# Input loads in turns, a second group of idle matmuls, and transposes tied between matmuls, in a two-layer SGU and retention trunk

## The chip, the cores and the metric

The kernel runs on one core of a Trainium2 chip. The metric is the device time of one execution in microseconds, as the median of three runs. One profiled execution of the same program gives the trace that is read here; its times are counted from the start of its span. PE is the matrix engine with its own weight loads beside it, DVE the vector engine, ACT the scalar engine, POOL the GpSimd engine, and SP the engine whose queue issues most DMAs.

## What is computed

A trunk of two layers over 512 rows (tokens) of 1024 columns in float32. Layer 0 mixes with a spatial gating unit, layer 1 with retention over four heads, and each is followed by a feed-forward layer (FFN) with SwiGLU of hidden width 2816. Every mixer and FFN sees a normed copy of the stream.

```python
def rmsnorm(x, g):
    return x * lax.rsqrt(jnp.mean(x * x, axis=-1, keepdims=True) + EPS) * g

def sgu_mixer(h, w_in, w_s, b_s, ln_g, ln_b, w_out):
    z = jax.nn.gelu(h @ w_in)
    u, v = jnp.split(z, 2, axis=-1)
    v = layernorm(v, ln_g, ln_b)
    ...                                    # causal mixing inside chunks of 128 rows
    return (u * mixed) @ w_out

def swiglu(h, w_gu, w_down):
    a, b = jnp.split(h @ w_gu, 2, axis=-1)
    return (jax.nn.silu(a) * b) @ w_down

def reference(x, ...):
    h = x
    for i in range(DEPTH):                 # DEPTH = 2
        hn = rmsnorm(h, mix_norm_g[i])
        h = h + (sgu_mixer(hn, ...) if i == 0 else retention(hn, ...))
        h = h + swiglu(rmsnorm(h, ffn_norm_g[i]), ffn_w_gu[i], ffn_w_down[i])
    return rmsnorm(h, final_norm_g)
```

## The kernel before

**Precision and tiles.** The 512 rows are four chunks `c` of 128. A float32 operand of a large matrix product is split into a high part, its value rounded to the matrix engine's fast float32 type (fp32r), and a low part, the rest. A product is then three matmuls into one sum: high times high, high times low, low times high (`three`, L246 to L249). For a weight tile (two blocks of 128 rows by 512 columns) `halves` (L209) makes the high part `wh_` on ACT (L216, L219) and the low part `wl_` on DVE (L223, L226) from the raw tile `wr_` that SP loads (`fetch_tile`, L201). In the first mixer these steps also multiply by the norm's weights, which have to stand as columns: `rows_to_cols` (L190) transposes rows by one matmul against an identity and copies the result on DVE. `mix0` is such a set of columns for the first norm, `gains` a set for later uses.

**Activations.** `turn` (L665) turns a chunk: eight transposes of 128 by 128 on PE (L669) into PSUM, then the high part `XH_` on ACT (L673) and the low part `XL_` on DVE (L674), both over 128 x 1024.

**Opening.** Five idle matmuls (`wake`, L176) run on PE before any data is there; the profile shows each as two instructions. Then x's chunks arrive in halves of 256 KB (`load_x`, L783), and the first product is `v0`, the first 512 columns of v: four steps `i` over pairs of blocks of the depth, four chunks `c`, each pair of `c` and step six matmuls of 512 columns, 96 in all. The products don't wait for the norm's factor per row: it is applied at the gelu (L827), so the squares of x (`square_in`, L787) and a chain of small DVE operations (`rsqrt_cols`) have to be done only by then. After v0 come v1, the other half of v, and u0 and u1.

**FFN.** Products of FFN and output are formed by a scheme with seven block products in place of eight (`seven`, L321), whose products P1, P7, P6, Q4, P5, P2, P3 run in an order given by hand. P1 and P7 come first; each needs a weight sum and an activation sum. In an FFN the raw weights of P6 come out of those of P7 by an accumulating DMA on POOL's queue, and then get their high and low parts like any tile. The first product, P1, needs chunks of rows that the norm before has only just made: with `between`, the job that turns the fourth chunk (`late_one`) runs behind step 0 of P1, and the jobs in `between` come behind P1's last step. `turn_late` (L689) turns a chunk with high priority.

**What sets the order.** `pipeline` runs a list of jobs and starts the loading, high and low steps of a job a fixed number of jobs ahead (FETCH 8, HIGH 6, PREP 5). A scheduler then orders each engine's instructions by their dependences and priority, so the order on an engine isn't that of the code; `tc.issue_after(instruction)` ties what stands in it behind an instruction. An engine takes its own instructions strictly in its order, and SP issues loads in its order.

The functions that the change touches, as they stand:

## Time and profile before

| what | us |
|---|---|
| median of three runs | 1203.94 |
| the runs, lowest to highest | 1203.91 to 1204.99 |
| the profiled execution | 1203.29 |
| its span (first to last instruction) | 1201.5 |
| PE busy | 1184.5 (99%) |
| DVE busy | 924.1 (77%) |
| ACT busy | 643.7 (54%) |
| POOL busy | 160.8 (13%) |

Busy time says how long an engine had an instruction in work, not whether it worked at full speed: matmuls are pipelined, and the granted clock (PEclk, as a share of the full 2.4 GHz; 0.50 is 1.2 GHz) is listed by stretch. A row of a timeline gives start, duration and instruction, and behind it in brackets how long the engine stood idle before it and what released it. Lines (L669) are those of the kernel before.

### The profile page before, as it was taken

The numbers are of one execution on the slowest core, as the hardware profiler recorded it, in microseconds if no ns is written. First come the engines' busy times: TensorE is split into PE (matmuls) and PEld (weight loads), VectorE is DVE, ScalarE is ACT, GpSimd is POOL, SyncE is SP. The second block draws the span as 40 slices with busy tenths as digits, with TensorE's granted clock in tenths as the row PEclk, the third lists the DMA queues.
The fourth block names the chain that finished last, engine by engine and source line by source line (L and its number), as shares of the span: only waits on it lengthen the run. The fifth ranks groups of instructions, "written<-read, shape, count | busy, mean of one in ns | idle before, by whom it ended". The sixth has DMA issues, their size and how long they took to land.

```text
span 1201.5 us, 18058 instructions
## 1 busy us (share of the span) xinstructions
PE 1184.5 (99%) x7206; PEld 1062.8 (88%) x7206; DVE 924.1 (77%) x1095; ACT 643.7 (54%) x815; POOL 160.8 (13%) x143
## 2 busy tenths in 40 slices
PE   8999999999999999999999999999999999999997
PEld 7888899998999988988888888888899989999986
DVE  5587968698987789787674757879768797666897
ACT  5523755454444547555453645566556554455465
POOL 1000120111110130201101001130121111101210
PEclk9999999999999999999999999999999999999999
DMA  9912968767876788766566457878866788677792
GB/s 314 281 52 54 246 133 206 180 162 216 203 204 145 202 176 266 182 139 172 115 186 145 120 132 170 205 129 282 220 140 173 180 223 221 153 192 191 151 243 99
DMA packets 118980, 216.42 MB, mean 180 GB/s; under 512 B 7496, under 2 KB 20848, under 8 KB 118896
## 3 DMA queue, kind: packets, MB, share of 16 engines
q1 hardware_dynamic: 83888, 148.13, 36.9%
q0 software_dynamic: 34720, 66.61, 33.1%
q8 instruction: 56, 0.92, 0.3%
q10 hardware_dynamic: 288, 0.52, 0.1%
q14 instruction: 28, 0.23, 0.1%
HBM read 212.10 MB, written 2.10 MB: 178 GB/s over the span
## 4 chain that ended last, share of the span: by engine, by line
PE 86%; issue 5%; DMA 4%; DVE 3%; ACT 2%; POOL 1%; SPq 0%; DVEq 0%; POOLq 0%; ACTq 0%
PE X_gu L249 6%; PE X_gu L248 6%; PE X_gu L247 6%; PE Y_gu L248 3%; PE Y_gu L249 3%; PE Y_gu L247 3%; PE X_dn L247 3%; PE X_dn L248 3%; PE X_dn L249 3%; PE X_vg L247 2%; PE X_vg L248 2%; PE X_vg L249 2%; PE ps_qk L247 2%; PE ps_qk L248 2%; PE ps_qk L249 2%
## 5 line engine op out<-in xcount | busy, mean ns | idle before, releaser
L223 DVE TENSOR_TENSOR wl_gu_P<-wr_gu_P,wh_gu_P 128x1024 fp32r<-128x1024 f32 x120 | 144.6, 1220 | 45.1 <-ACT wh_gu_P L216 44.9
L216 ACT ACTIVATE wh_gu_P<-wr_gu_P 128x1024 fp32r<-128x1024 f32 x120 | 122.7, 1052 | 66.2 <-DVE wr_gu_P L375 34.7
L347 POOL DMA_DIRECT2D wr_gu_P<-in_ffn_w_gu x48 | 58.4, 1258 | 381.3 <-DMA wr_gu_P<-in_ffn_w_gu 167.3
L216 ACT ACTIVATE wh_dn_P<-wr_dn_P 128x1024 fp32r<-128x1024 f32 x72 | 69.3, 981 | 51.7 <-DMA wr_dn_P<-in_ffn_w_down 13.3
L223 DVE TENSOR_TENSOR wl_vg_P<-wr_vg_P,wh_vg_P 128x1024 fp32r<-128x1024 f32 x48 | 58.3, 1220 | 34.9 <-ACT wh_vg_P L216 28.7
L223 DVE TENSOR_TENSOR wl_dn_P<-wr_dn_P,wh_dn_P 128x1024 fp32r<-128x1024 f32 x72 | 79.5, 1130 | 3.2 <-issue 2.2
L347 POOL DMA_DIRECT2D wr_vg_P<-in_ret_w_in x26 | 31.5, 1250 | 262.7 <-DMA wr_vg_P<-in_ret_w_in 79.2
L347 POOL DMA_DIRECT2D wr_dn_P<-in_ffn_w_down x36 | 42.0, 1242 | 179.5 <-DMA wr_dn_P<-in_ffn_w_down 92.3
L216 ACT ACTIVATE wh_vg_P<-wr_vg_P 128x1024 fp32r<-128x1024 f32 x48 | 49.6, 1055 | 28.5 <-DMA wr_vg_P<-in_ret_w_in 13.6
L248 PE MATMUL ps_qk<-XL_r,wh_qk 128*128 128x512 f32 (+1 forms) x160 | 55.6, 348 | 0.0
L247 PE MATMUL ps_qk<-XH_r,wh_qk 128*128 128x512 f32 (+1 forms) x160 | 55.3, 348 | 0.0
L249 PE MATMUL ps_qk<-XH_r,wl_qk 128*128 128x512 f32 (+1 forms) x160 | 55.1, 348 | 0.0
L248 PE MATMUL Y_gu<-xP7l_f,wh_gu_P 128*128 128x256 f32 x160 | 45.4, 284 | 0.4 <-DVE xP7l_f L743 0.4
L248 PE MATMUL X_gu<-XL_f,wh_gu_P 128*128 128x256 f32 x160 | 45.4, 283 | 0.0
L249 PE MATMUL X_gu<-XH_f,wl_gu_P 128*128 128x256 f32 x160 | 45.3, 283 | 0.0
L247 PE MATMUL X_gu<-xP6h_f,wh_gu_P 128*128 128x256 f32 x160 | 45.3, 283 | 0.0
L248 PE MATMUL X_gu<-xP6l_f,wh_gu_P 128*128 128x256 f32 x160 | 45.3, 283 | 0.0
L249 PE MATMUL X_gu<-xP6h_f,wl_gu_P 128*128 128x256 f32 x160 | 45.3, 283 | 0.0
L247 PE MATMUL Z_gu<-XH_f,wh_gu_P 128*128 128x256 f32 x160 | 45.3, 283 | 0.0
L248 PE MATMUL Z_gu<-XL_f,wh_gu_P 128*128 128x256 f32 x160 | 45.3, 283 | 0.0
L249 PE MATMUL Z_gu<-XH_f,wl_gu_P 128*128 128x256 f32 x160 | 45.3, 283 | 0.0
L247 PE MATMUL X_gu<-xP5h_f,wh_gu_P 128*128 128x256 f32 x160 | 45.3, 283 | 0.0
(590 smaller groups left out, 4206.8 us busy)
## 6 DMA issues: line engine op xcount, KB each, us to landing
wr_gu_P<-in_ffn_w_gu SPq DMA_DIRECT2D x100, 512.0 KB, 4.8
wr_dn_P<-in_ffn_w_down SPq DMA_DIRECT2D x50, 512.0 KB, 4.9
wr_gu_P<-in_ffn_w_gu POOLq DMA_DIRECT2D x48, 512.0 KB, 7.6
wr_vg_P<-in_ret_w_in SPq DMA_DIRECT2D x40, 512.0 KB, 5.0
wr_dn_P<-in_ffn_w_down POOLq DMA_DIRECT2D x30, 512.0 KB, 7.4
wr_vg_P<-in_ret_w_in POOLq DMA_DIRECT2D x26, 512.0 KB, 7.4
wr_ro_P<-in_ret_w_out SPq DMA_DIRECT2D x20, 512.0 KB, 5.6
wr_qk<-in_ret_w_in SPq DMA_DIRECT2D x32, 256.0 KB, 3.1
```

Source lines behind the costliest of these rows:

```text
L216: nc.scalar.activation(h, s, AF.Copy)
L223: nc.vector.tensor_tensor(l, s, f32(h), ALU.subtract)
L247: nc.tensor.matmul(o, ah, bh, start=start, stop=False, skip_group_check=True)
L248: nc.tensor.matmul(o, ah, bl, start=False, stop=False, skip_group_check=True)
L249: return nc.tensor.matmul(o, al, bh, start=False, stop=stop, skip_group_check=True)
L347: nc.gpsimd.dma_start(raw[p, 0, g, s][:, 0:nk, :], source(b, g, s, nk), accum_op=ALU.add)
```

## The change

It does five things.

- In the opening, x's chunks and v0's weight tiles are issued on SP in turns: chunk 0, tile 0, chunk 1, tile 1, and so on, in sixteen DMAs of 256 KB. Before, tile 0 came behind chunk 0, then came chunks 1 to 3, and tiles 1 to 3 followed behind another small load, as three DMAs of 512 KB.
- Ten more idle matmuls (WAKE2) are tied behind the transpose of the `mix0` weights.
- In v0's loop the order in the code changes: a step turns its chunk first, takes the earlier tiles for it, and then the new tile for all chunks so far.
- All four squares are made on ACT behind that loop. Before, the first was made on DVE, and each stood in the loop.
- In `seven`, with `between`, the matmuls of P1's step 1 for the first chunk of a pair are tied behind the last transpose that `turn` issued. This holds in both FFNs.

```diff
+WAKE2 = 10
...
+    def keep_awake(n, after=None):
+
+        wake = PS("wake")
+        for _ in range(n):
+            with tc.issue_after(after.ins) if after else nullcontext():
+                after = nc.tensor.matmul(wake[:, 0, 0:P], ones, ones, start=True, stop=True)
+        done(wake)
+
+    keep_awake(WAKE)
...
-        nc.tensor.transpose(ps[:, 0, 0:n], rows_in[name], ident[0:n, 0:n])
+        xn["turned"] = nc.tensor.transpose(ps[:, 0, 0:n], rows_in[name], ident[0:n, 0:n])
...
                 for c in range(2):
-                    matmuls(p, g, s, nk, c)
+                    with tc.issue_after(xn["turned"].ins) if between and i == 1 and c == 0 else nullcontext():
+                        matmuls(p, g, s, nk, c)
...
-            nc.tensor.transpose(ps[:, k, :], src[:, k * P:(k + 1) * P], ident)
+            xn["turned"] = nc.tensor.transpose(ps[:, k, :], src[:, k * P:(k + 1) * P], ident)
...
     def square_in(c):
-        sq = G(f"xq{c}", F32, (P, D))
-        if c == 0:
-            nc.vector.scalar_tensor_tensor(sq, X[:, c, :], 1.0, X[:, c, :], ALU.mult, ALU.mult, accum_out=ss2[:, c:c + 1])
-        else:
-            nc.scalar.activation(sq, X[:, c, :], AF.Square, accum_out=ss2[:, c:c + 1])
+        nc.scalar.activation(G(f"xq{c}", F32, (P, D)), X[:, c, :], AF.Square, accum_out=ss2[:, c:c + 1])
 
     load_rows(nc.gpsimd, "mix0", mix_g[0:1])
-    load_x(0)
-    v0w = [None] * NC
-    wr = G("wr_v0_0")
-    for a in range(2):
-        nc.sync.dma_start(wr[:, a, :], w_in[a * P:(a + 1) * P, D:D + T])
+    raw0 = []
+
+    def load_w0(kp):
+        raw0.append(G(f"wr_v0_{kp}"))
+        for a in range(2):
+            k = 2 * kp + a
+            nc.sync.dma_start(raw0[kp][:, a, :], w_in[k * P:(k + 1) * P, D:D + T])
+
+    for what, i in ((load_x, 0), (load_w0, 0), (load_x, 1), (load_w0, 1), (load_x, 2), (load_w0, 2), (load_x, 3), (load_w0, 3)):
+        what(i)
+    done(turn(0, X[:, 0, :], "in"))
     mix0_col = rows_to_cols("mix0")
-    done(turn(0, X[:, 0, :], "in"))
+    keep_awake(WAKE2, xn["turned"])
     vps = [PS(f"ps_v0_{i}") for i in range(2)]
+    v0w = []
     for i in range(NC):
         if i > 0:
-            wr = fetch_tile(f"v0_{i}", w_in, 2 * i, 2, ((D, T),))
-        if i + 1 < NC:
-            load_x(i + 1)
-        v0w[i], high, low = halves(wr, f"v0_{i}", 2, [mix0_col(2 * i + a) for a in range(2)])
+            done(turn(i, X[:, i, :], "in"))
+            for kp in range(i):
+                natural_step(vps[i // 2][:, i % 2, :], i, kp, v0w[kp])
+        parts, high, low = halves(raw0[i], f"v0_{i}", 2, [mix0_col(2 * i + a) for a in range(2)])
         high()
         low()
-        for c in range(i):
+        v0w.append(parts)
+        for c in range(i + 1):
             natural_step(vps[c // 2][:, c % 2, :], c, i, v0w[i])
-        for kp in range(i + 1):
-            natural_step(vps[i // 2][:, i % 2, :], i, kp, v0w[kp])
-        square_in(i)
-        if i + 1 < NC:
-            done(turn(i + 1, X[:, i + 1, :], "in"))
+    for c in range(NC):
+        square_in(c)
```

What that makes of the engines' orders is shown at three places. In these rows `x8` counts like instructions in a row, and a name's last number tells one buffer from another.

PE at the very start, before the change. `xT_in_0` to `xT_in_3` are the transposes of x's four chunks, `mix0_ps` that of the norm's weights, `ps_v0_0` and `ps_v0_1` the sums of v0, `wh_v0_0` and `wl_v0_0` the parts of its first weight tile:

```order
L176 MATMUL wake_89<-ones_81 128x128 x5
L669 MATMUL xT_in_0_108<-ident_76,X_95 128x128 x8
L193 MATMUL mix0_ps_104<-ident_76,mix0_rows_97 128x8
L669 MATMUL xT_in_1_139<-ident_76,X_95 128x128 x8
L247 MATMUL ps_v0_0_121<-wh_v0_0_125,XH_in_117 128x512
L669 MATMUL xT_in_2_180<-ident_76,X_95 128x128 x8
L248 MATMUL ps_v0_0_121<-wl_v0_0_126,XH_in_117 128x512
```

And with the change:

```order
L181 MATMUL wake_89<-ones_81 128x128 x5
L677 MATMUL xT_in_0_119<-ident_76,X_95 128x128 x8
L200 MATMUL mix0_ps_132<-ident_76,mix0_rows_97 128x8
L181 MATMUL wake_136<-ones_81 128x128 x10
L677 MATMUL xT_in_1_161<-ident_76,X_95 128x128 x8
L254 MATMUL ps_v0_0_147<-wh_v0_0_149,XH_in_128 128x512
L677 MATMUL xT_in_2_196<-ident_76,X_95 128x128 x4
L255 MATMUL ps_v0_0_147<-wl_v0_0_150,XH_in_128 128x512
```

The ten idle matmuls stand ahead of the second chunk's transposes. The first four transposes of the third chunk still stand behind one matmul of v0, as all eight did.

DVE around the gains, before the change (`wl_v0_1` to `wl_v0_3` are low parts of v0's tiles, `gains_cols` the columns of the gains):

```order
L226 SCALAR_TENSOR_TENSOR wl_v0_1_155<-wr_v0_1_150,mix0_cols_106,wh_v0_1_154 128x512 x2
L195 COPY gains_cols_331<-gains_ps_329 128x32
L674 TENSOR_TENSOR XL_in_118<-xT_in_3_233,XH_in_117 128x8x128
L226 SCALAR_TENSOR_TENSOR wl_v0_2_196<-wr_v0_2_191,mix0_cols_106,wh_v0_2_195 128x512 x2
L226 SCALAR_TENSOR_TENSOR wl_v0_3_247<-wr_v0_3_244,mix0_cols_106,wh_v0_3_246 128x512 x2
```

With the change, on DVE:

```order
L621 TENSOR_TENSOR dg0_n0_570<-ident_76,ch_n0_565 128x512
L621 TENSOR_TENSOR dg1_n0_573<-ident_76,cl_n0_567 128x512
L202 COPY gains_cols_345<-gains_ps_343 128x32
L233 SCALAR_TENSOR_TENSOR wl_v1_0_387<-wr_v1_0_370,mix0_cols_134,wh_v1_0_386 128x512 x2
L233 SCALAR_TENSOR_TENSOR wl_v1_1_391<-wr_v1_1_372,mix0_cols_134,wh_v1_1_390 128x512 x2
```

and on PE, where v0 ends:

```order
L255 MATMUL ps_v0_1_148<-wl_v0_3_273,XH_in_128 128x512
L256 MATMUL ps_v0_1_148<-wh_v0_3_272,XL_in_129 128x512
L200 MATMUL gains_ps_343<-ident_76,gains_rows_339 128x32
L254 MATMUL ps_v1_0_430<-wh_v1_0_386,XH_in_128 128x512
L254 MATMUL ps_v1_1_431<-wh_v1_0_386,XH_in_128 128x512
L255 MATMUL ps_v1_0_430<-wl_v1_0_387,XH_in_128 128x512
```

The copy of the gains stands on DVE directly ahead of v1's low parts, and their transpose on PE between v0's last matmul and v1's first. Before, both stood in v0's first half.

ACT in the first FFN, before the change (`wh_gu0_0_P6_0_0` is the high part of P6's first weight tile, `xT_f0_1` the turned fourth chunk, `xr_` raw copies of a turned chunk, `s1_` a later combination of sums):

```order
L216 ACTIVATE wh_gu0_0_P6_0_0_1494<-wr_gu0_0_P722_0_0_1246 128x1024
L673 ACTIVATE XH_f0_1270<-xT_f0_1_1563 128x8x128
L216 ACTIVATE wh_gu0_0_P6_0_2_1527<-wr_gu0_0_P722_0_2_1284 128x1024
L216 ACTIVATE wh_gu0_0_P2_0_0_1559<-wr_gu0_0_P221_0_0_1497 128x1024
L1025 ACTIVATE s1_0_0_1600<-X_gu0_0_1532 128x1024
L706 ACTIVATE xr_f0_0_0_1464<-xT_f0_1_1563 128x4x128
L706 ACTIVATE xr_f0_0_1_1465<-xT_f0_1_1563 128x4x128
```

With the change:

```order
L223 ACTIVATE wh_gu0_0_P6_0_0_1508<-wr_gu0_0_P722_0_0_1260 128x1024
L681 ACTIVATE XH_f0_1284<-xT_f0_1_1577 128x8x128
L223 ACTIVATE wh_gu0_0_P6_0_2_1541<-wr_gu0_0_P722_0_2_1298 128x1024
L714 ACTIVATE xr_f0_0_0_1478<-xT_f0_1_1577 128x4x128
L714 ACTIVATE xr_f0_0_1_1479<-xT_f0_1_1577 128x4x128
L223 ACTIVATE wh_gu0_0_P2_0_0_1573<-wr_gu0_0_P221_0_0_1511 128x1024
L1034 ACTIVATE s1_0_0_1614<-X_gu0_0_1546 128x1024
```

The raw copies moved ahead of P2's high part; XH of the fourth chunk stands behind P6's first high part in both. On PE the chunk's eight transposes moved ahead of P1's step 1.

## Rows read from the trace of the kernel before

**Rows 1.** The page, part 1: engine, busy us (share of the span), instructions.

```profile
PE 1184.5 (99%) x7206; PEld 1062.8 (88%) x7206; DVE 924.1 (77%) x1095; ACT 643.7 (54%) x815; POOL 160.8 (13%) x143
```

**Rows 2.** Waits of PE, whole span: total us, times, longest us.

```profile
PE xT_in L669 <- DMA X<-in_x: 2.9, 2, 2.7
...
PE ps_gl L247 <- ACT XH_f L673: 1.0, 1, 1.0
PE ps_gl L248 <- DVE XL_f L674: 1.0, 1, 1.0
```

**Rows 3.** Busy time by stretch: bounds, length, engines (instructions), PEclk, DMA, GB/s.

```profile
4.64:8.06 3.42, 0.85 (x7) 0.59 (x5) 1.80 (x3) 2.37 (x3) 0.00 (x0) 1.00 0.84 275
8.06:11.47 3.41, 3.27 (x15) 3.12 (x16) 2.30 (x5) 1.04 (x2) 0.00 (x0) 0.50 1.06 374
```

**Rows 4.** Timeline, PE in the opening: start, duration, instruction, [idle before <-releaser].

```profile
1.21 2.50 PE L176 MATMUL wake<-ones 128*128 128x128 f32 x10 [1.21 <-POOL eps L170]
...
5.27 0.23 PE L193 MATMUL mix_ps<-ident,mix_rows 8*128 8x8 f32 x1
...
8.20 1.94 PE L669 MATMUL xT_in<-ident,X 128*128 128x128 f32 x8 [2.70 <-DMA X<-in_x]
...
13.06 0.50 PE L247 MATMUL ps_v<-wh_v,XH_in 128*128 128x512 f32 x1 [0.42 <-ACT XH_in L673]
...
16.43 0.24 PE L193 MATMUL gains_ps<-ident,gains_rows 32*128 32x32 f32 x1
```

**Rows 5.** Chain that ended last, opening: start us, us, what.

```profile
2.67 5.39 DMA X<-in_x
8.06 0.14 issue
...
14.25 0.87 PE xT_in L669 x8
```

**Rows 6.** Timeline, SP's queue: the ninth input DMA, first half of x's fourth chunk.

```profile
4.57 0.67 SPq L785 DMA_DIRECT2D X<-in_x  x1
```

**Rows 7.** DMA issues, same transfer: count, KB, us to landing.

```profile
X<-in_x SPq DMA_DIRECT2D x1, 256.0 KB, 6.5
```

**Rows 8.** Timeline, PE where v0's matmuls end and v1's begin.

```profile
34.23 0.39 PE L248 MATMUL ps_v<-wl_v,XH_in 128*128 128x512 f32 x1
...
35.37 0.62 PE L247 MATMUL ps_v<-wh_v,XH_in 128*128 128x512 f32 x2
35.82 0.39 PE L248 MATMUL ps_v<-wl_v,XH_in 128*128 128x512 f32 x1
```

**Rows 9.** Timeline, DVE: the gains' copy, its next instruction, v1's first low halves.

```profile
16.71 0.19 DVE L195 COPY gains_cols<-gains_ps 128x32 f32<-128x32 f32 x1 [1.13 <-PE gains_ps L193]
16.82 1.22 DVE L674 TENSOR_TENSOR XL_in<-xT_in,XH_in 128x1024 fp32r<-128x1024 f32 x1
...
27.07 1.41 DVE L226 SCALAR_TENSOR_TENSOR wl_v<-wr_v,mix_cols,wh_v 128x512 fp32r<-128x512 f32 x2 [1.87 <-ACT wh_v L219]
```

**Rows 10.** Timeline, ACT: gelu of v0, the first use of the norm factors.

```profile
39.47 2.40 ACT L827 ACTIVATE v<-ps_v,ry_n 128x512 f32<-128x512 f32 x4
```

**Rows 11.** Timeline, PE in the first FFN, at P1's end.

```profile
168.73 1.04 PE L669 MATMUL xT_f<-ident,xs_f 128*128 128x128 f32 x8
...
171.36 0.50 PE L247 MATMUL ps_gl<-XH_f,wh_gl 128*128 128x256 f32 x2 [1.01 <-ACT XH_f L673]
172.84 0.39 PE L248 MATMUL ps_gl<-XL_f,wh_gl 128*128 128x256 f32 x1 [0.98 <-DVE XL_f L674]
```

**Rows 12.** Timeline, ACT and DVE in the same stretch.

```profile
169.34 1.06 ACT L216 ACTIVATE wh_gu_P<-wr_gu_P 128x1024 fp32r<-128x1024 f32 x1 [3.92 <-DMA wr_gu_P<-in_ffn_w_gu]
...
170.30 1.00 ACT L673 ACTIVATE XH_f<-xT_f 128x1024 fp32r<-128x1024 f32 x1
170.43 1.23 DVE L223 TENSOR_TENSOR wl_gu_P<-wr_gu_P,wh_gu_P 128x1024 fp32r<-128x1024 f32 x1 [5.00 <-ACT wh_gu_P L216]
...
171.57 1.22 DVE L674 TENSOR_TENSOR XL_f<-xT_f,XH_f 128x1024 fp32r<-128x1024 f32 x1
```

More of the change, by code (lines that the diff above doesn't have):

```diff
@@ L173, in trunk @@
     nc.scalar.activation(const.tile([P, 1], F32, name="first"), ones[:, 0:1], AF.Gelu_apprx_tanh)
-    wake = PS("wake")
-    for _ in range(WAKE):
-        nc.tensor.matmul(wake[:, 0, 0:P], ones, ones, start=True, stop=True)
-    done(wake)
+    def keep_awake(n, after=None):
[5 more added lines that the diff above has]
+    keep_awake(WAKE)
     rows_in = {}
```

## The prediction, made before the change was run

> **What bounds the kernel now.** I began with the page: PE is busy 1184.5 of 1201.5 us [rows 1], so a change is worth what it takes from or adds to PE's own time and idle time, and the other engines count only where PE waits for them. The list of PE's waits comes next. It has few entries, and the two places that the change touches are among them: 2.9 us for x in the opening, and twice 1.0 us, each once, for the parts XH and XL of the fourth chunk in a feed-forward layer [rows 2]. The table of stretches then gives the clock: PE had little to do up to 8.06 (0.85 us of work), and in the next 3.41 us it worked 3.27 us at a granted clock of 0.50, the lower of its two levels, 1.2 GHz [rows 3]. The eight transposes of 8.20 take 1.94 us there; the eight of the fourth chunk, later and at the full clock, take 0.87 us, 0.109 each [rows 4, 5]. After that PE runs without a break until v1: seven matmuls from 34.23 to 35.82 are 0.227 us apart [rows 8]. I therefore compare both kernels at one point, the first matmul of v1 that needs a low half (35.82 before): whatever moves it moves the rest, since everything behind it is again bound by PE.
>
> **Opening: the loads.** Bytes and the count of transfers up to x's last half stay as the list of the change gives them; the order changes. The second weight tile now comes ahead of x's third chunk. PE's queue still has that chunk's transposes behind a single matmul, so PE can't use the early weights: it stands until the third chunk's first half is there. That half is now SP's ninth input transfer. The ninth one before (first half of the fourth chunk) was issued at 4.57 and took 6.5 us, landing at 11.1 [rows 6, 7]; the eight ahead of it have 256 KB each in both kernels, so I take 11.1, give or take 0.3. PE starts 0.14 us after a landing (8.06 to 8.20 [rows 4, 5]), so at 11.2. Before it, the second chunk (landing at 8.06) and one matmul are done by about 9.5, and PE idles some 1.7 us that it did not idle before.
>
> From 11.2 there is work without a gap: 16 transposes at 0.109 make 1.74 us, and 95 of v0's 96 matmuls at 0.227 make 21.57 us. v0 ends at 34.5. Later weights and chunks are hidden: the last of the sixteen input transfers comes at the place where the last v0 tile came before, and PE needs the fourth chunk only behind more than ten matmuls.
>
> **Opening: the idle matmuls.** Five of them show as ten instructions in 2.50 us at the slow clock [rows 4]. Ten are twenty instructions, 2.5 us at the full clock and 5.0 us at half. They start when the norm weights' transpose ends, at 5.5, and so end between 8.0 and 10.5, ahead of 11.2 either way. Their cost is nothing, and so is their gain: transposes that run faster from 8.2 on only lengthen the wait for the third chunk.
>
> **Opening: squares and gains.** The first square goes from DVE to ACT, and all four stand behind the weights' high parts, two of them ahead of the fourth chunk's XH. That makes the norm factors perhaps 2 us later; their first use is the gelu at 39.47 [rows 10], and the fourth chunk's first matmul stands at about 25. Nothing is late. The transpose of the gains is another matter. It moves from the middle of v0 (16.43 [rows 4]) to behind v0's last matmul, and its copy on DVE now stands **ahead of v1's first low halves**. Before, those were made at 27.07, 8 us before they were wanted [rows 9]. Now DVE, in order, sits idle until the transpose has run, and behind the copy are queued all low halves of v1 and u0. PE is the one that waits: transpose at 34.5, copy 0.28 later, next DVE instruction 0.11 after its start (16.43, 16.71, 16.82 [rows 4, 9]), one low half 0.71 (1.41 for two), hand-over to PE 0.05 (171.57 + 1.22 to 172.84 [rows 11, 12]): 35.65. A first matmul after a wait takes some 0.1 longer (0.50 in place of 0.39 [rows 8, 11]): 35.8. Before it was 35.82. The opening gives **0.0 us**. Without the new wait the same matmul would come at 34.5 plus the transpose (0.2) and two matmuls (0.45), so at 35.2, a gain of 0.6. Behind this point DVE has eight low halves to catch up, 5.6 us, while PE takes 24 matmuls, 5.4 us, for every two of them.
>
> **The tie.** In the first feed-forward layer the fourth chunk's eight transposes start 24 matmuls earlier or nearly so, at about 166.5 in place of 168.73 [rows 11]. But XH and XL don't follow from the transposes alone. On ACT, XH stands behind the high part of P6's first weight tile in both orders, and that one starts at 169.34, after 3.92 us of waiting for its DMA; XH follows at 170.30. On DVE, XL stands behind the low part of the same tile (170.43) and follows at 171.57 [rows 12]. Neither start is set by PE. So PE reaches the first matmul that reads XH as early as before, waits until 171.36 and again until 172.84 [rows 11], and the tie gains **0.0 us** of the 2.0 that its idle time shows, or of some 2.4 with a slow start behind each wait. In the second layer the transposes move by two matmuls, and the waits for XH and XL happen only once in the run [rows 2], so nothing is there to win. The two raw copies that now stand ahead of another high part on ACT have over 10 us in hand.
>
> **The clock.** [rows 3, 4] show the lower level only after a wait of 2.70 us behind 0.85 us of work. The Trainium skill (TensorE: Matmul & The Clock Gate, Part 1, What's actually happening) says that the throttled clock is the default, that activity releases it, and that the number of slow matmuls differs from run to run. By that rule, the slow stretch of this profile need not be in the timed runs of the kernel before. I weigh that below as a rival.
>
> **Sum.** Opening 0.0, tie 0.0. The profiled execution took 1203.29 (span 1201.5), the median is 1203.94, 0.65 more; I carry the difference to the median: 1203.9 us. The terms' own uncertainty is 0.3 for the landing and 0.2 for the DVE chain: 1203.3 to 1204.5.
>
> **Rivals.**
> A clock that falls (the slower side): the new idle time of about 1.7 us, from 9.5 to 11.2, lets the granted clock drop. What speaks for it is the drop behind 2.70 us; what speaks against it is that the new one is shorter, nearer to the two idle times of 1.0 us [rows 2] around which PE's clock stays full. It decides from the point at which a stretch like that of [rows 3], 3.41 us at 0.50, begins after 11.2: half of it, 1.7 us, is lost, 1205.6, and with a third chunk that lands 0.8 us later 1206.4.
> The tie works: if P6's DMA comes early enough, or XH isn't held, 2.0 to 2.4 us go: 1201.5 to 1201.9. Against it stands the order on ACT.
> The gains' copy doesn't hurt, because the low halves come sooner than I add up: 0.6 us gained, 1203.3.
> The slow stretch is not in the timed runs of before. Then before doesn't pay for it, up to about 0.8 us (half of the 1.94 us of transposes of 8.20, less what the arrival of x gives back), and the change, which idles anyway, is that much slower: 1204.7. Against it: the profiled run, with the stretch, is faster than all three timed ones.
>
> **How the numbers follow.** Forecast 0.55, clock 0.17, tie works 0.11, copy hidden 0.12, slow stretch absent 0.05. About 0.2% (2.4 us) is what a measurement of this kernel tells from no change. The forecast, the hidden copy and the absent stretch all lie within it; of the clock's 0.17 some 0.06 pass 1206.3, and with 0.03 for what I don't see slower has 0.09; of the tie's 0.11 somewhat over half passes 1201.5, faster 0.07. The rest, 0.84, is no change. The range leaves out the tie and the clock's far end, some 17 in 100: from 1202.6 (0.7 below the hidden copy: 0.3 of the landing, 0.2 of the chain, 0.2 for the spread of the runs) to 1206.3.
>
> **What would show it.** The third chunk's transposes start at 11.0 to 11.5 behind an idle PE; earlier than 10.5 and the loads are misjudged. PE's clock is full from 11.5 on; 0.50 there is the first rival. The gains' transpose stands at about 34.5, and behind it PE waits some 0.4 us for DVE's low half of v1; if that wait is missing, the copy was hidden. Near 170 the fourth chunk's transposes stand 2.3 us earlier against P1's matmuls, while PE still waits about 1 us each for XH and XL; if those two waits are gone from the list, the tie works and the forecast is wrong by over 2 us.

## The result, and the profile after the change

| | us |
|---|---|
| before, median of 20 runs (lowest to highest) | 1205.00 (1202.81 to 1207.38) |
| changed, median of 20 runs | 1206.24 (1204.12 to 1208.65) |
| ratio of changed to before, 95% interval | 1.0017 (1.0011 to 1.0024) |
| the same kernels compared once more, 11 and 29 runs | 1.0014 (1.0005 to 1.0022) |
| profiled execution of the changed kernel, its span | 1204.12, 1202.3 |

The change makes the kernel slower by about 0.15%. The medians give 1.2 and 0.9 us in the two comparisons, the ratios 2.0 and 1.7, and the means of all 31 runs of the change and all 118 of before 1.4, give or take 0.5; below, 1.4 stands for it. That is less than the 0.2% that the prediction set as its bound, but it is clear of zero, where the forecast was no change. The kernel before is slower than it looked too: its median over 20 runs is 1.1 us above that of the three runs that were known. So of the 2.3 us between the forecast of 1203.9 and 1206.24 about half is the change.

The page, part 1, and PE's waits over the whole span of the changed kernel (us in total, times, longest):

```profile
PE 1185.6 (99%) x7226; PEld 1063.5 (88%) x7226; DVE 922.3 (77%) x1093; ACT 644.5 (54%) x817; POOL 160.8 (13%) x143
```
```profile
PE xT_in L677 <- DMA X<-in_x: 2.3, 2, 1.3
PE ps_gl L254 <- ACT XH_f L681: 1.3, 1, 1.3
...
PE Y_gu L255 <- DVE xP7l_f L751: 1.0, 1, 1.0
PE ps_gl L255 <- DVE XL_f L682: 1.0, 1, 1.0
```

PE is busy 1.1 us longer than before [rows 1], with twenty more instructions, the idle matmuls. In the opening two waits for x, 2.3 us in all, stand where 2.9 were, nearly all of it in one [rows 2]. The waits for XH and XL are still there, as forecast. New in size is the wait for **xP7l, the low part of P7's activation sum**, 1.0 us in the second FFN. In the kernel before it was this one:

```profile
893.21 0.39 PE L248 MATMUL Y_gu<-xP7l_f,wh_gu_P 128*128 128x256 f32 x1 [0.36 <-DVE xP7l_f L743]
```

The opening on PE (start, duration, instruction, idle before and its releaser):

```profile
5.65 0.66 PE L677 MATMUL xT_in<-ident,X 128*128 128x128 f32 x4 [1.07 <-DMA X<-in_x]
...
6.39 2.50 PE L181 MATMUL wake<-ones 128*128 128x128 f32 x20
8.73 1.10 PE L677 MATMUL xT_in<-ident,X 128*128 128x128 f32 x8
9.58 0.47 PE L254 MATMUL ps_v<-wh_v,XH_in 128*128 128x512 f32 x1
11.33 0.63 PE L677 MATMUL xT_in<-ident,X 128*128 128x128 f32 x4 [1.27 <-DMA X<-in_x]
11.71 0.47 PE L255 MATMUL ps_v<-wl_v,XH_in 128*128 128x512 f32 x1
```

The third chunk's transposes stand behind an idle PE at 11.33, where the prediction put 11.2. From there the timeline has no gap until v0 ends. The granted clock is at the upper level, 2.4 GHz, from 4.59 on (stretches: bounds, length, busy time of PE, PEld, DVE, ACT, POOL, then PEclk):

```profile
4.59:8.06 3.47, 2.41 (x20) 2.22 (x20) 0.82 (x2) 1.71 (x3) 0.00 (x0) 1.00 0.88 265
8.06:11.47 3.41, 2.14 (x19) 1.78 (x18) 2.44 (x4) 2.13 (x4) 0.00 (x0) 1.00 1.05 401
11.47:14.88 3.41, 3.41 (x20) 2.90 (x20) 3.30 (x5) 2.88 (x5) 0.00 (x0) 1.00 1.00 364
```

Where v0 ends and v1 begins, PE and then DVE:

```profile
34.50 0.39 PE L256 MATMUL ps_v<-wh_v,XL_in 128*128 128x512 f32 x1
34.82 0.24 PE L200 MATMUL gains_ps<-ident,gains_rows 32*128 32x32 f32 x1
35.00 0.85 PE L254 MATMUL ps_v<-wh_v,XH_in 128*128 128x512 f32 x2
36.01 0.50 PE L255 MATMUL ps_v<-wl_v,XH_in 128*128 128x512 f32 x1 [0.17 <-DVE wl_v L233]
36.35 0.39 PE L256 MATMUL ps_v<-wh_v,XL_in 128*128 128x512 f32 x1
```
```profile
35.11 0.19 DVE L202 COPY gains_cols<-gains_ps 128x32 f32<-128x32 f32 x1 [9.34 <-PE gains_ps L200]
35.21 2.06 DVE L233 SCALAR_TENSOR_TENSOR wl_v<-wr_v,mix_cols,wh_v 128x512 fp32r<-128x512 f32 x3
```

The gains' transpose runs at 34.82, behind v0's last matmul. Its copy on DVE starts at 35.11, the low half directly behind it at 35.21, and PE takes up that half at 36.01 after an idle stretch of 0.17 and a slow pair of matmuls (0.85 in place of 0.62 [rows 8]). The prediction put this at 35.8; before it was 35.82.

In the first FFN, PE and then ACT:

```profile
166.78 1.04 PE L677 MATMUL xT_f<-ident,xs_f 128*128 128x128 f32 x8
...
172.00 0.50 PE L254 MATMUL ps_gl<-XH_f,wh_gl 128*128 128x256 f32 x2 [1.32 <-ACT XH_f L681]
173.48 0.39 PE L255 MATMUL ps_gl<-XL_f,wh_gl 128*128 128x256 f32 x1 [0.98 <-DVE XL_f L682]
```
```profile
169.98 1.06 ACT L223 ACTIVATE wh_gu_P<-wr_gu_P 128x1024 fp32r<-128x1024 f32 x1 [4.24 <-DMA wr_gu_P<-in_ffn_w_gu]
170.94 1.01 ACT L681 ACTIVATE XH_f<-xT_f 128x1024 fp32r<-128x1024 f32 x1
```

The transposes of the fourth chunk stand at 166.78, ahead of 24 matmuls of P1, and PE has P1 done by 170.7, against 170.35 before (171.36 less the wait of 1.01 [rows 11]). XH still stands behind the high part of P6's first tile, which waits for its DMA until 169.98. So the two waits of [rows 11] are there again, the first one even longer, 1.32 in place of 1.01.

### The profile page after: what moved, and what is told of

Read it like the earlier page. It is cut to its first block, busy times and chain, and to the rows that moved or that the text cites. A ratio compares the mean times of both kernels' runs of the same rounds, so it can differ in the third digit from the quotient of the medians.

```text
span 1202.3 us, 18102 instructions
## 1 busy us (share of the span) xinstructions
PE 1185.6 (99%) x7226; PEld 1063.5 (88%) x7226; DVE 922.3 (77%) x1093; ACT 644.5 (54%) x817; POOL 160.8 (13%) x143
## 5 line engine op out<-in xcount | busy, mean ns | idle before, releaser
L254 PE MATMUL X_gu<-XH_f,wh_gu_P 128*128 128x256 f32 x160 | 45.4, 284 | 0.0
L256 PE MATMUL Y_gu<-XH_f,wl_gu_Q 128*128 128x256 f32 x160 | 45.3, 283 | 0.0
L254 PE MATMUL Y_gu<-XH_f,wh_gu_Q 128*128 128x256 f32 x160 | 45.3, 283 | 0.0
L255 PE MATMUL Y_gu<-XL_f,wh_gu_Q 128*128 128x256 f32 x160 | 45.3, 283 | 0.0
L256 PE MATMUL X_gu<-xP3h_f,wl_gu_P 128*128 128x256 f32 x160 | 45.3, 283 | 0.0
L255 PE MATMUL X_gu<-xP5l_f,wh_gu_P 128*128 128x256 f32 x160 | 45.3, 283 | 0.0
```

The lines of the kernel that those rows point to most:

```text
L254: nc.tensor.matmul(o, ah, bh, start=start, stop=False, skip_group_check=True)
L255: nc.tensor.matmul(o, ah, bl, start=False, stop=False, skip_group_check=True)
L256: return nc.tensor.matmul(o, al, bh, start=False, stop=stop, skip_group_check=True)
```

## Experiments

### Is the order on ACT and DVE what makes the tie worthless?

**tie_only**: the kernel before with the last of the change's five parts alone.

```diff
                 for c in range(2):
-                    matmuls(p, g, s, nk, c)
+                    with tc.issue_after(xn["turned"].ins) if between and i == 1 and c == 0 else nullcontext():
+                        matmuls(p, g, s, nk, c)
...
-            nc.tensor.transpose(ps[:, k, :], src[:, k * P:(k + 1) * P], ident)
+            xn["turned"] = nc.tensor.transpose(ps[:, k, :], src[:, k * P:(k + 1) * P], ident)
```

> The kernel before with the tie alone (fourth chunk's transposes between P1's steps); opening as before. Theory A (the opening makes the change slower, the tie does nothing, since XH and XL stand behind P6's first tile on ACT and DVE): within 0.4 us of before, ratio 0.9997 to 1.0003, and PE still waits about 1.0 us each for XH and XL near 171 to 173. Rival B (the tie itself costs, by later raw copies or a later accumulate DMA): over 1 us slower, ratio 1.0008 or more. Rival C (the tie gains and the opening hides it): 2.0 to 2.4 us faster, ratio 0.998.

Measured: 1204.40 against 1205.16, ratio 0.9994 (0.9984 to 1.0004). In its profile PE waits 1.17 us for XH and 0.98 for XL. The tie alone does nothing that can be measured; rivals B and C are out. (The profiled execution is the slowest of tie_only's runs, 1208.94; what it shows beside these waits comes below.)

**hold** and **hold_tie** take away what stands ahead of XH. The high and low parts of P6's two tiles are issued behind P7's activation sum, in both FFNs. hold has no tie, hold_tie has it.

```diff
             def high():
...
-                high_()
+                if held is not None and p == "P6":
+                    held.append((high_, rest_low))
+                else:
+                    high_()
...
+        def let_go():
+            xparts("P6", ask=True)
+            while held:
+                high_, low_ = held.pop(0)
+                with tc.issue_after(xn["P7", "h"].ins):
+                    high_()
+                with tc.issue_after(xn["P7", "l"].ins):
+                    low_()
...
-                  mid={("h", 0): lambda: xparts("P5", ask=True), ("h", 1): lambda: xparts("P6", ask=True),
+                  mid={("h", 0): lambda: xparts("P5", ask=True), ("h", 1): let_go,
```

> The kernel before (no tie, opening as before), but the high and low parts of P6's two weight tiles in both FFNs' first unit are held back behind P7's activation sum, so that the fourth chunk's XH and XL no longer stand behind a DMA on ACT and DVE. Theory (the waits near 171 and 173 come from P6's first tile ahead of XH and XL): the transposes stay at 168.7, XH starts at 169.6, XL at about 170.6; PE waits 0.3 for XH and 1.1 for XL in place of 1.0 and 1.0, 0.6 us gained there, and in the second FFN the wait of 0.4 to 1.7 us for xP7l goes. In all 1 to 2.5 us, ratio 0.998 to 0.9992. Rival (XH and XL are late because the transposes are): waits as before, ratio 0.9995 to 1.0005.

> As the kernel hold, with the tie. Theory: with nothing ahead of XH, the tie now pays: transposes at 166.8, XH at 167.7, XL done by 170.0, P1's matmuls last until 170.5, so no wait of PE for XH or XL: 2.0 to 2.4 us from the FFN's waits, and up to 1.7 us more where the lower clock followed those waits (it did near 173 to 179 in four of the last four profiles), 0.4 to 1.7 in the second FFN: ratio 0.9960 to 0.9980. Rival (the tie is worth nothing even so): ratio as for hold, 0.998 to 0.9992.

Measured: hold 1203.06 against 1204.58, ratio 0.9986 (0.9977 to 0.9994); hold_tie 1201.32 against 1204.58, ratio 0.9973 (0.9963 to 0.9983), and once more, as **hold_tie_2**, 1200.97 against 1205.19, ratio 0.9965 (0.9952 to 0.9977).

PE in the first FFN with hold:

```profile
169.41 1.04 PE L676 MATMUL xT_f<-ident,xs_f 128*128 128x128 f32 x8
...
171.56 0.50 PE L247 MATMUL ps_gl<-XH_f,wh_gl 128*128 128x256 f32 x2 [0.53 <-ACT XH_f L680]
172.81 0.39 PE L248 MATMUL ps_gl<-XL_f,wh_gl 128*128 128x256 f32 x1 [0.76 <-DVE XL_f L681]
```

With nothing ahead of XH but the late transposes, the waits shrink from 1.0 and 1.0 to 0.53 and 0.76. With the tie as well they are gone. ACT and DVE in hold_tie:

```profile
168.18 1.02 ACT L681 ACTIVATE XH_f<-xT_f 128x1024 fp32r<-128x1024 f32 x1 [2.09 <-PE xT_f L677]
169.10 1.05 ACT L216 ACTIVATE wh_gu_P<-wr_gu_P 128x1024 fp32r<-128x1024 f32 x1
...
175.62 1.04 ACT L216 ACTIVATE wh_gu_P<-wr_gu_P 128x1024 fp32r<-128x1024 f32 x1
```
```profile
169.24 1.22 DVE L682 TENSOR_TENSOR XL_f<-xT_f,XH_f 128x1024 fp32r<-128x1024 f32 x1 [3.14 <-ACT XH_f L681]
```

XH follows the transposes at once (168.18 in place of 170.30 [rows 12]), P6's high parts come at 175.62, XL ends at 170.5, and PE's list of waits has no XH, XL or xP7l:

```profile
PE xT_in L677 <- DMA X<-in_x: 2.6, 1, 2.6
PE wake L176 <- POOL eps L170: 1.2, 1, 1.2
PE pv L248 <- DVE vl L1169: 0.7, 1, 0.7
PE X_vg L247 <- ACT xr_r L714: 0.5, 1, 0.5
```

So the prediction's step on the tie was right, and the gain that its rival gave the tie exists: hold_tie lies 2.0 us below hold (means of 13 and 11 runs, 1201.28 and 1203.33). It needs the place on ACT and DVE that P6's first tile held.

### What do the parts of the opening cost?

**opening_only**: the change without its tie. **nowake2**: the change with `WAKE2 = 1`. **gains_early**: the change with the gains' transpose and copy inside v0's last step:

```diff
+    load_rows(nc.gpsimd, "gains", ret_gn_g, sgu_ln_g, sgu_ln_b)
...
             done(turn(i, X[:, i, :], "in"))
+            if i == 3:
+                gain_col = rows_to_cols("gains")
...
-    load_rows(nc.gpsimd, "gains", ret_gn_g, sgu_ln_g, sgu_ln_b)
-    gain_col = rows_to_cols("gains")
```

**gains_late**: the kernel before with the reverse, its gains tied behind v0's last matmul:

```diff
-            natural_step(vps[i // 2][:, i % 2, :], i, kp, v0w[kp])
+            last = natural_step(vps[i // 2][:, i % 2, :], i, kp, v0w[kp])
...
-    gain_col = rows_to_cols("gains")
+    with tc.issue_after(last.ins):
+        gain_col = rows_to_cols("gains")
```

**before_wake**: the kernel before with ten idle matmuls behind the `mix0` transpose and ahead of the second chunk; this also puts v0's first matmul ahead of that chunk, and the third chunk's transposes directly behind the second's. **ungate_gains**: gains_early, and the third chunk's transposes behind v0's first six matmuls in place of one:

```diff
-            done(turn(i, X[:, i, :], "in"))
+            with tc.issue_after(own[0].ins) if i == 2 else nullcontext():
+                done(turn(i, X[:, i, :], "in"))
...
-            natural_step(vps[c // 2][:, c % 2, :], c, i, v0w[i])
+            own.append(natural_step(vps[c // 2][:, c % 2, :], c, i, v0w[i]))
```

> The changed kernel without the tie: loads in turns, ten idle matmuls, squares on ACT, v0's new order. Theory A: as slow as the whole change, ratio 1.0013 to 1.0023, runs with a lower mean clock being the slow ones (0.999 near 1204.3, 0.996 near 1207.8). Rival B (the tie costs): ratio 1.000 to 1.0008. Rival C: ratio over 1.003.

> The changed kernel with one idle matmul behind the norm weights' columns in place of ten. Theory A1 (in executions that still run at the lower clock there, twenty idle instructions take 5.0 us in place of 2.5 and push the second chunk's transposes from 8.7 to about 11): the slow end of the runs falls, median 1 to 2 us under that of the whole change, ratio to before 1.000 to 1.0008. Rival A2 (the idle matmuls keep the clock up, and without them PE has 2 us more of idle time): mean clock falls below the whole change's 0.997, median 1 us or more above it, ratio 1.0025 or more. Rival A3 (they do nothing): ratio 1.0013 to 1.0023 as with them.

> The whole change with the gains' transpose and copy inside v0's loop instead of behind it, so that v1's low halves stand ready. Theory A (the copy behind v0's end costs PE the time from 35.0 to 36.0 at v1's start): v1's first matmul with a low half about 0.6 to 0.8 us earlier, at 35.2 to 35.4, and the median 0.6 us under that of the whole change, ratio to before 1.0008 to 1.0018. Rival (DVE's low halves are late anyway, since their tiles land at 27 and later): no difference from the whole change, a wait at v1's start of the same size.

> The kernel before with one thing of the change: the gains' transpose and copy behind v0's last matmul. It takes 0.24 us of PE's time out of v0 and puts it behind. Theory (the copy on DVE holds v1's low halves and costs by itself what moving it back gave in the changed kernel): v1's first matmul with a low half 0.6 to 0.9 us later than in the kernel before, ratio 1.0003 to 1.0009. Rival (it is the changed v0 order that is slow at v1): ratio 0.9997 to 1.0002.

> The kernel before with the ten idle matmuls behind the norm weights' columns and ahead of the second chunk (v0's first matmul comes ahead of that chunk with it). Theory (in the kernel before, the first matmuls wait for DMA, ACT and DVE until about 13, so a clock of 0.50 there costs it little, and keeping the clock up gives little): mean clock up by 0.001, ratio 0.9995 to 1.0003. Rival (the slow stretch costs it 1 to 2 us): ratio 0.998 to 0.9992.

> The whole change, with the gains' copy inside v0 and the third chunk's transposes behind the first chunk's six matmuls instead of behind one. Theory (the opening's cost is PE standing for the third chunk's first half with work at hand, and the copy): five matmuls of 0.227 run in the wait of 1.27 us, 1.1 us gained, and the copy's 0.6; v1's first matmul with a low half at 34.2 to 34.6 at the full clock, ratio to before 0.9978 to 0.9995. Rival (what is gained in the opening is lost to lower clock or to DVE's low halves): v1's low half at 35.2 or later, ratio 0.9998 to 1.001.

| kernel | median, us | ratio to before (95%) |
|---|---|---|
| opening_only | 1205.91 | 1.0004 (0.9995 to 1.0013) |
| nowake2 | 1206.63 | 1.0017 (1.0007 to 1.0028) |
| gains_early | 1205.42 | 1.0001 (0.9993 to 1.0010) |
| gains_late | 1205.57 | 1.0007 (0.9997 to 1.0017) |
| before_wake | 1204.72 | 0.9999 (0.9990 to 1.0008) |
| ungate_gains | 1204.65 | 1.0002 (0.9993 to 1.0011) |

These intervals are about 1 us wide to either side, as large as what is looked for. opening_only decides neither way. The profiles say more, but each is one execution.

**The gains' copy.** In gains_early x's third chunk lands as in the changed kernel (11.18 and 11.19), the clock is full in both, and v1 begins without a wait:

```profile
35.14 0.62 PE L254 MATMUL ps_v<-wh_v,XH_in 128*128 128x512 f32 x2
35.59 0.39 PE L255 MATMUL ps_v<-wl_v,XH_in 128*128 128x512 f32 x1
35.82 0.39 PE L256 MATMUL ps_v<-wh_v,XL_in 128*128 128x512 f32 x1
```

The matmul behind the first low half stands at 35.82 in place of 36.35, so the copy costs 0.53 us at v1's start, in a comparison of two profiles. The runs agree that there is a price and don't fix its size. gains_early lies 1.0 us below the change, give or take 0.6 (means of 11 and 31 runs, which weren't taken side by side), so that with the copy moved little of the change's loss is left. gains_late is above the kernel before by less than its interval, and in its profile v1's first low half stands at 38.53 with a second chunk that landed 1.7 us later (9.80), so that profile prices nothing. A third pair of kernels (hold_gains, below) shows no gain, give or take 1.6.

**The lower clock in the opening.** Of the changed opening opening_only has a stretch at 0.50 in the middle of v0 (and v1 at its start, on PE):

```profile
8.30:11.71 3.41, 1.69 (x11) 1.23 (x12) 1.89 (x3) 2.11 (x4) 0.00 (x0) 1.00 1.05 397
11.71:15.13 3.42, 3.42 (x13) 2.83 (x12) 2.64 (x4) 1.96 (x4) 0.00 (x0) 0.51 1.05 369
```
```profile
37.81 0.50 PE L255 MATMUL ps_v<-wl_v,XH_in 128*128 128x512 f32 x1 [0.16 <-DVE wl_v L233]
```

There v1's first low half comes at 37.81, 1.8 us behind the 36.01 of the changed kernel, while the third chunk landed only 0.19 later. That is near the price that the first rival was given, 1.7. nowake2 has the lower level from about 8.6 to 15.5, over v0's first matmuls:

```profile
8.69:15.52 6.83, 5.74 (x22) 4.55 (x21) 4.41 (x6) 5.46 (x8) 0.00 (x0) 0.51 1.07 384
```

Its ratio is that of the change, as A3 had it. Its mean clock falls, 0.996 in place of 0.997, as A2 had it, and the mean of its runs lies 1.0 us above that of the change, give or take 0.9; in its profile PE stands at v1 1.9 us behind the kernel before. So the ten idle matmuls seem to be worth something to the changed opening. The old opening takes such a stretch for little: before_wake keeps the full clock from 4.75 on (mean clock of its runs 0.998 against 0.996), yet gains nothing by its runs, and v1 starts there 0.2 us later than in the kernel before, with a second chunk that landed 0.46 later, so by these two profiles the stretch costs the old opening some 0.3. There PE's first matmuls wait for x, ACT and DVE anyway.

**The third chunk.** In ungate_gains the wait of 1.27 us is filled as planned, and v1 stands 1.1 us earlier than in the kernel before. Its runs don't show a gain; its profile has the waits for XH, XL and xP7l at 1.23, 0.98 and 1.34.

### Where do the 1.4 us lie?

By their runs' mean clock the two kernels behave differently. The changed kernel's 31 runs lie near 1204.6 at 0.999 (5 runs), 1206.2 at 0.997 (14), 1207.9 at 0.996 (8): 0.9 us for each 0.001, by a straight line through them. The 99 runs of before that have a clock beside them lie near 1204.7 at 0.999 (3), 1205.0 at 0.997 (25), 1204.8 at 0.996 (32), 1204.7 at 0.995 (11), 1206.1 at 0.994 (14): 0.2 us. That speaks for a lower clock that costs the changed kernel more, not yet for its place. **change_again** and **change_3** to **change_6** are the changed kernel, unedited, for further profiles.

> The changed kernel as it is, for a second profile and more runs. Theory (at the full clock the change costs nothing, and its slower median comes from stretches at 0.50 which now fall on an opening in which PE has no gaps): runs with a mean clock of 0.999 near 1204.7, those of 0.996 near 1207.8, about 1 us for each 0.001, while the runs of the kernel before show no such slope between 0.999 and 0.995. Rival (the extra time is spread over waits that have nothing to do with the clock): no slope, and runs of 0.999 as slow as the rest, near 1206.4.

> A further profile of the changed kernel, for the clock alone. Theory (the change's slower median comes from stretches at 0.50 in the opening, where PE now has work without a gap from 11.2 on): in about half of the profiles a stretch at 0.50 reaches beyond 11.5, and there v1's first matmul with a low half stands 1.3 to 1.9 us later than at 36.0. Rival (the opening stays at the full clock from 6 on, as in two profiles of two so far, and the stretches come only behind the FFNs' waits, as in the kernel before): 35.9 to 36.3 in every profile.

> A further profile of the changed kernel, with the same two cases as change_3: a stretch at 0.50 beyond 11.5 and v1's first low half 1.3 to 1.9 us after 36.0 in about half of the profiles, or 35.9 to 36.3 in all.

> A further profile of the changed kernel, with the same two cases as change_3: a stretch at 0.50 beyond 11.5 and v1's first low half 1.3 to 1.9 us after 36.0 in about half of the profiles, or 35.9 to 36.3 in all.

> A further profile of the changed kernel, with the same two cases as change_3: a stretch at 0.50 beyond 11.5 and v1's first low half 1.3 to 1.9 us after 36.0 in about half of the profiles, or 35.9 to 36.3 in all.

Measured: change_again 1205.99 against 1205.11, ratio 1.0014 (1.0005 to 1.0022); change_3 to change_6, one execution each, 1206.11, 1205.64, 1204.68 and 1206.11. For each profile, how much later PE stands than at the same matmuls of the kernel before (medians over all matmuls in a stretch, worked out from the traces), the waits, and from issue to landing the accumulate DMA that stands ahead of each: that of P6's first tile in the first FFN (DMA 1) and of P6's second tile in the second FFN (DMA 2).

| profile | at v1 (36) | at 180 | at 870 | at 900 | wait XH | DMA 1 | wait xP7l | DMA 2 | 0.50 at 173 to 178 |
|---|---|---|---|---|---|---|---|---|---|
| before | 0 | 0 | 0 | 0 | 1.01 | 5.68 | 0.36 | 7.44 | no |
| changed | 0.33 | 0.63 | 0.26 | 0.92 | 1.32 | 6.00 | 1.02 | 8.11 | no |
| change_again | 0.27 | 1.76 | 1.34 | 2.49 | 1.12 | 5.80 | 1.51 | 8.60 | yes |
| change_3 | 0.17 | 2.27 | 2.01 | 2.94 | 1.64 | 6.30 | 1.29 | 8.38 | yes |
| change_4 | 0.88 | 2.39 | 1.73 | 2.45 | 1.04 | 5.71 | 1.06 | 8.15 | yes |
| change_5 | 0.58 | 0.63 | 0.70 | 1.48 | 1.06 | 5.73 | 1.14 | 8.23 | no |
| change_6 | 0.43 | 2.27 | 2.04 | 3.01 | 1.37 | 6.05 | 1.32 | 8.41 | yes |

Each wait is its DMA's time less a constant: 4.67 us for XH, 7.09 for xP7l, to within 0.02 in every row. The seven other profiles with these waits fit too, but for tie_only's second (9.00, wait 1.66). So a longer wait here is a longer transfer, and nothing else.

The opening is at the full clock in six of six, as the rival of change_3 said (v1's first low half comes at 35.85 to 36.54, a little beyond its range). But the six have mean clocks of 0.997 to 0.999; none is of an execution at 0.996 or below, where nine of the 31 timed runs lie, the slowest among them. What those lose, and where, no profile of the change shows. The profiles of the kernels closest to it that were taken at 0.994 to 0.996 have two stretches at 0.50 each: opening_only and nowake2 one in the opening and one behind XH and XL, tie_only one behind XH and XL and one behind xP7l. In the six the lower level stands elsewhere than in the opening, in four of them: **behind the two waits of the first FFN**. In change_6, stretches, and the waits on PE ahead of it:

```profile
171.40:174.80 3.40, 1.67 (x11) 1.46 (x12) 2.19 (x2) 0.70 (x1) 1.20 (x1) 0.99 0.95 172
174.80:178.20 3.40, 3.40 (x18) 3.40 (x17) 1.03 (x1) 2.12 (x4) 0.00 (x0) 0.51 0.94 155
178.20:181.60 3.40, 3.40 (x31) 3.40 (x30) 3.40 (x4) 3.40 (x4) 2.46 (x2) 1.00 0.25 30
```
```profile
172.16 0.51 PE L254 MATMUL ps_gl<-XH_f,wh_gl 128*128 128x256 f32 x2 [1.37 <-ACT XH_f L681]
173.64 0.39 PE L255 MATMUL ps_gl<-XL_f,wh_gl 128*128 128x256 f32 x1 [0.98 <-DVE XL_f L682]
```

PE was busy 1.67 of 3.40 us around its two waits, and in the next 3.40 us it did 18 matmuls where the following stretch has 31. Between 172 and 180 that costs 1.47 us there (PE stands 0.80 us behind the kernel before once it has both parts, and 2.27 behind at 180). Of the four kernels with the old opening and these waits, tie_only and gains_late show the same stretch, the kernel before and before_wake don't. So it isn't new with the change, and four of six and two of four can't be told apart.

The second place is the second FFN. There xP7h and xP7l stand on ACT and DVE behind P6's second tile, which waits for its DMA. ACT and PE in change_again:

```profile
884.97 1.06 ACT L223 ACTIVATE wh_gu_P<-wr_gu_P 128x1024 fp32r<-128x1024 f32 x1 [1.84 <-DMA wr_gu_P<-in_ffn_w_gu]
888.79 2.01 ACT L223 ACTIVATE wh_gu_P<-wr_gu_P 128x1024 fp32r<-128x1024 f32 x2 [2.76 <-DMA wr_gu_P<-in_ffn_w_gu]
...
892.55 1.05 ACT L748 ACTIVATE xP7h_f<-xP_f 128x1024 fp32r<-128x1024 f32 x1
```
```profile
895.71 0.39 PE L255 MATMUL Y_gu<-xP7l_f,wh_gu_P 128*128 128x256 f32 x1 [1.51 <-DVE xP7l_f L751]
```

Before, that DMA landed at 886.28, 7.4 us after its issue, and PE waited 0.36; here it landed at 888.77, 8.6 after its issue, and PE waits 1.51. All six profiles of the change have 1.02 to 1.51. That isn't new with the change either: of the four kernels with the old opening, before_wake (1.33) and tie_only (1.66) wait as long, the kernel before (0.36) and gains_late (0.44) don't. In tie_only this wait too is followed by the lower clock, 0.50 from 897.93 to 901.34, which costs it about 1.5 us more:

```profile
897.39 0.38 PE L248 MATMUL Y_gu<-xP7l_f,wh_gu_P 128*128 128x256 f32 x1 [1.66 <-DVE xP7l_f L744]
```

**hold_change** (the whole change with P6's parts held back), hold_tie_2 and **hold_gains** (hold_change with the gains' copy inside v0) take these waits away on either opening:

> The whole change with P6's parts held back, so that neither FFN has a wait of PE, nor the lower clock behind one: against hold_tie_2 it differs in the opening alone. Theory A (the opening with the gains' copy behind v0 costs nothing, as predicted; the change's slower median comes from the lower clock behind the FFN's waits): within 0.5 us of hold_tie_2, ratio to before 0.9968 to 0.9978. Theory B (the opening costs the 1.4 us): 1.0 to 1.8 us slower than hold_tie_2, ratio to before 0.9980 to 0.9990.

> The kernel hold_tie once more (opening of before, the tie, P6's parts held back), on the same chip as hold_change: ratio to before 0.9966 to 0.9980, the runs within 2 us of each other, since the lower clock has no wait of the FFNs to follow and costs the opening little.

> As hold_change, with the gains' copy inside v0. Theory A (the copy costs what the profiles show at v1's start): 0.5 to 0.6 us under hold_change. Theory B (it costs the 1.0 us that the timed runs of gains_early suggest): 0.8 to 1.2 us under it.

| kernel | median, us | ratio to before (95%) |
|---|---|---|
| hold_change | 1200.35 | 0.9962 (0.9950 to 0.9975) |
| hold_tie_2 | 1200.97 | 0.9965 (0.9952 to 0.9977) |
| hold_gains | 1201.42 | 0.9971 (0.9959 to 0.9983) |

Theory B is out, and theory A holds: with the FFNs' waits gone, the changed opening is not slower than the old one (0.6 us faster by the medians, within the scatter of five runs each). Mean of hold_change less mean of all 13 runs of hold_tie is -0.6, give or take 1.2, so of the 1.4 us at most some 0.6 can lie in the opening by itself. hold_gains is no faster than hold_change, which neither of its theories had; the copy's 0.5 us stays a reading of profiles.

The traces say the same of the opening. The eight profiles with the changed opening (the six, opening_only and hold_change) stand at v1 0.2 to 2.1 us behind the one of the kernel before, 0.6 in the mean. The five with the old one (before, tie_only, hold, hold_tie and hold_tie_2) stand there at 0 to 1.5, 0.6 in the mean.

### The best of the parts

**best**: the change with gains' copy inside v0, the third chunk's transposes behind six matmuls, and P6's parts held back.

> The whole change with all of it: gains' copy early, third chunk's transposes later, P6's parts held back. Theory: the gains add: 3 to 6 us faster than before, ratio 0.9950 to 0.9975, and no wait of PE over 0.8 us is left behind the opening. Rival (PE meets the next late thing, xP6l or a P6 low part near 190): 1 to 2 us, ratio 0.9983 to 0.9992.

Measured: 1199.16 against 1204.58, ratio 0.9957 (0.9944 to 0.9971), 5 us faster than the kernel before, and the fastest kernel of this study by its median; hold_change isn't told apart from it. What PE still waits for (us in total, times, longest):

```profile
PE wake L181 <- POOL eps L171: 1.2, 1, 1.2
PE pv L255 <- DVE vl L1181: 0.7, 1, 0.7
PE xT_in L685 <- DMA X<-in_x: 0.7, 1, 0.7
```

## Why the prediction went wrong, step by step

- **Loads: right.** The ninth transfer landed at 11.19 (forecast 11.1, give or take 0.3) and PE followed at 11.33 (11.2). The idle time ahead of it was 1.27 where the prediction said 1.7, since the second chunk landed at 8.43 in place of 8.06. In the six profiles PE starts that chunk between 11.17 and 11.87.
- **v0's end and the gains' copy: right, short by 0.2.** 36.01 for v1's first low half where the sum said 35.8. The sum took 34.5 for the end of v0; that is where its last matmul starts, and the gains' transpose starts at 34.82. The wait itself is 0.17 where some 0.4 was expected; the rest went into the slow pair of matmuls ahead of it.
- **Idle matmuls, squares.** They cost nothing that shows, as forecast; no run takes the squares apart. That the idle matmuls gain nothing is in doubt: without them (nowake2) the lower clock lasts until 15.5 in the one profile, PE stands at v1 1.9 behind the kernel before in place of 0.2 to 0.9, and the runs are 1.0 us slower in the mean, give or take 0.9.
- **The tie: right, and shown by hold_tie.** XH and XL were held by P6's first tile, not by the transposes.
- **The opening as a whole: not contradicted.** 0.0 forecast; hold_change against hold_tie_2 says -0.6, give or take a bit over 1, and the profiles at v1 show no difference.
- **The clock in the opening: price right, and rare in the profiles.** The rival's 1.7 us is near what opening_only shows (1.8), but the stretch was there in one of the eight profiles with this opening, and in none of the six of the change. The Trainium skill (TensorE: Matmul & The Clock Gate, Part 1, What's actually happening) served for the rival by which the slow stretch of [rows 3] need not be in the timed runs. In the five other profiles with the old opening (tie_only, hold, hold_tie, hold_tie_2, gains_late) the slow transposes are there too; only before_wake, which fills the wait, is without them. So that rival falls. As the Trainium skill says there, the number of slow matmuls differs from run to run: here they last until 11.5 in the kernel before and 15.7 in gains_late.
- **What failed: the sum, "Opening 0.0, tie 0.0", as the whole of the change.** It took every wait behind v1 at the size that one profile shows and asked only whether the change takes it away. On the second layer it said that "nothing is there to win"; that the wait for xP7l there, 0.36 in that profile, could grow was not costed at all. In six of six profiles of the change it is 1.02 to 1.51. The waits for XH and XL were costed at 2.0 with nothing behind them, and named as idle times "around which PE's clock stays full"; in four of six profiles a stretch at 0.50 follows and costs 1.4 to 1.5 more there, of which 0.8 to 1.3 is left at 870. Take the waits away (hold_change), and the change's loss is gone; that is why the loss is put to these places and not to the opening alone. How much of it each place carries is not shown, nor that they are worse than in the kernel before, of which there is one profile. A second step that was off is the chance of the first rival, 0.17 for a clock that falls: it asked after the opening's new wait alone.
- **The starting point was low too.** The profile of before was one of its fast executions, 1203.29, with the shortest wait for xP7l seen here, and its median over 20 runs is 1205.00. Carrying 0.65 to the median of three runs carried less than half of the 1.71 that was needed.

What stays open: **why** the changed kernel meets longer waits in the second FFN, or the lower clock in the first more often, than the kernel before. Or whether it does: neither part alone shows it. tie_only is level with before, opening_only has 1.0004 with an interval that takes in both zero and the 1.4 us. The DMA behind xP7l's wait took 7.4 us in some executions and over 8 in others, in kernels with the tie (nowake2 waits 0.43) and without it (opening_only waits 1.47, before_wake 1.33). A count of profiles large enough to tell such shares apart was not made. A rival also stands in part: gains_early, which moves nothing but the gains' copy, is 1.0 us below the change, give or take 0.6, so the copy may carry a good part of the loss (0.5 us by the profiles). hold_change bounds the opening as a whole to some 0.6, and with it the copy, unless something else in the opening gains.

## What to carry to other kernels

Where PE waits for a result of ACT or DVE, look at what stands ahead of the wanted instruction there, and at what that waits for, before moving anything upstream. Here the transposes moved by 2 us and gained nothing (ratio 0.9994), and moving the neighbour too gained 3 to 4 us (hold_tie). And when two kernels are 0.1% apart, one profile of each can't carry the comparison: take each wait's spread over several executions, and take the waits away to see which stage holds the difference.

## What the runs showed of the hardware

- A clock stretch at 0.50 came in the middle of a kernel that had kept PE busy for some 160 us: two waits of 1.0 to 1.6 us and 0.98 us, 0.5 us apart, were followed by one in nine of the fourteen profiles that have these waits, at a cost of 1.4 to 1.5 us there. The single wait of 1.2 us for the third chunk was followed by one in opening_only, and in none of the six profiles of the change; the single wait for xP7l was followed by one in tie_only (1.66 us), and in none of the others (up to 1.51).
- The same stretch costs 1.8 us where PE has work without a gap (opening_only) and some 0.3 where PE waits for its inputs (the old opening, before against before_wake).
- The accumulate DMA of P6's second tile in the second FFN takes 7.4 to 7.5 us from issue to landing in three of the fourteen profiles and 8.1 to 9.0 in the others, and PE's wait for xP7l follows it: 0.36 to 0.44 in the three, 1.02 to 1.66 in the others. The wait for XH follows that of P6's first tile in the first FFN in the same way: 5.68 to 6.30 us, and 4.67 less.
